# Running streams: rotary queries and new rows padded with zeros to 128 rows, the latent product's heads by turns, the short-conv state stored in one piece

## The chip, the cores and the metric

The kernel runs on one core of one Trainium2 chip. The metric is device time in microseconds (us), from the first to the last instruction with what the launch adds around them; a median of runs stands for a kernel. The core has five engines with their own instruction queues: TensorE (PE in the rows; PEld is its weight load), VectorE (DVE), ScalarE (ACT), GpSimd (POOL) and SyncE (SP), and 16 DMA engines that all queues share.

## The reference, cut to what matters

Two layers of a streaming encoder. Each has three token mixers beside each other (latent attention, a Conformer convolution, a short gated convolution), merged by gates, then an MLP. There are 512 tokens of a new stream (the prompt) and 8 running streams with 16 new tokens each; a running stream attends to 512 cached keys and its own 16 new ones:

```
q_lat = einsum('bqhd,chd->bqhc', q_nope, w_uk)                 # the latent product
s = (einsum('bqhc,bkc->bhqk', q_lat, ckv) + einsum('bqhr,bkr->bhqk', q_rope, krope)) * scale
p = softmax(s)
o_lat = einsum('bhqk,bkc->bqhc', p, ckv)                       # 512 cached rows + 16 new rows
z = gc * h;  new_sc = concat(past_sc, z)[:, -2:]               # state of the short convolution
```

With 8 heads and 16 tokens, a running stream has 128 queries. A query has 256 latent numbers and 32 rotary numbers. `new_sc` are the last two rows of 256 channels, for the prompt and for each of the 8 running streams: 9 x 2 numbers for a channel.

## The kernel before, in words

All activations lie with channels on the 128 partitions. A matmul contracts over partitions: the stationary operand is loaded as weights, the moving one streams through. Dense products are split in a high and a low fp32r part and done in three matmuls (`mm3`, lines 430 to 446: high by high, high by low, low by high, lines 437, 439, 441). Plain fp32 matmuls (values, transposes) count as two instructions each.

Weights come through `Stream` (line 175): a group of up to 512 KB is loaded by SP (line 204), cut by ACT into `wh` (line 226) and by DVE into `wl` (line 227). One group is loaded ahead of the one in use.

The part around the change is the stage of the running streams, once in each layer: 186 to 285 us in layer 0 and from about 1182 us in layer 1. Before it come the prompt's 32 attention steps (loop of line 850). The last 8 of these also do `absorb` (line 821), the latent product: 16 plain matmuls with 64 rows, one at each `yield`, two yields in a step with a transpose between them. Four of them fill one bank of PSUM (`o`, line 829); the fourth is followed by a split of the bank by ACT and DVE into the two parts of `qlh` and `qll`.

In the stage the order of PE is the order of the code, and so is SP's; ACT, DVE and POOL are ordered by a planner that simulates the program, where functions marked `first` have precedence. For each stream b:

- `score_s(b)` (line 923): two halves of 264 keys. Each half takes nine matmuls: six over 128 rows (the two latent halves) and then three over 32 rows, the rotary part. The rotary queries of four streams lie on the four bands of 32 partitions of one tile (`qsr`, split at line 971 into `qsrh` and `qsrl`), and the matmul takes the band of stream b of the queries and of the rotary keys (`rg`, line 927). Then maximum (DVE), exponential (ACT), normalisation (DVE).
- `turn_s(b)` (line 943): transposes of the probabilities, into a tile `spT` of five blocks; the fifth has only 16 rows, for the new keys.
- `value_s(b)` (line 956): for two halves of the latent channels, four matmuls over 128 cached rows (line 962) and one over the 16 new rows (line 963) from `cnew`, a tile of 16 partitions that `new_rows` (line 914) fills for two streams.
- `cut_keys(b)` (line 891): splits the loaded keys (`kT`, `kR`) into two parts and starts the load for stream b + 2; `rows_of` (line 884) loads the value rows `kM`.

Between them run "fills": steps of the dense products `gc1`, `h1`, `gb0`, `gb1` (`side_tile`, line 575). A tile has two halves of eight steps, and a half takes the only bank `D0` of this stage; it is read out by ACT (line 591) or DVE (lines 596, 598, 600) before the next half begins. A stream has 3 fills before `turn_s` and 5 after it. 8 fills come ahead of the loop, after `score_s(0)`, so the order at the start is `score_s(0)`, half of `gc1`, `score_s(1)`, the other half of `gc1`.

`side_out` (line 588) also stores the short-conv state: when a tile `h` is done (for c = 0 just ahead of the stage, for c = 1 within it), POOL issues two DMAs from `Z` (lines 608 and 609), one for the prompt (2 numbers on each partition) and one for the running streams (8 pieces of 2 numbers on each partition).

Of the kernel before, what the change touches and what calls it, by code (L numbers as in the profile page):

```python
# [19 lines left out]
P = 128  # L20
D = 1024
KT = D // P
SEQ = 512
# [297 lines left out]
def trunk(tc, A, O):  # L321
# [54 lines left out]
    def split(h, lo, src, scale=None):  # L376

        return (nc.scalar.activation(out=h, in_=src, func=AF.Copy),
                nc.vector.tensor_tensor(out=lo, in0=src, in1=R(h), op=ALU.subtract))
# [19 lines left out]
    def mm_tile(name, n=HF, ps="D0"):  # L399
        b = banks[ps]  # L400
        return (b[0] if ps == "op" else b).tile([P, 512], F32, tag="mm", name=name)[:, :n]
# [42 lines left out]
    def mm3(*a, **k):  # L444
        for _ in mm3_steps(*a, **k):
            pass
# [61 lines left out]
    for l in range(DEPTH):  # L508
# [48 lines left out]
        Z = pf.tile([P, 2, 2 + SEQ + NB * (2 + NQ)], F32, name="Z")  # L557
        ZP = Z[:, :, 0:2 + SEQ]
        ZS = Z[:, :, 2 + SEQ:].rearrange("p c (b n) -> p c b n", b=NB)

        nc.gpsimd.memset(U[:, :, 0:CH], 0.0)
        nc.gpsimd.memset(Z[:, :, 0:2], 0.0)
# [25 lines left out]
        def side_out(n, c, i, a, b, t, o):  # L588
            q = lambda z: z[:, SEQ:].rearrange("p (b q) -> p b q", b=NB)
            if n == "ca" or n == "gc":  # L590
                nc.scalar.activation(out=t[:, a:b], in_=o, func=AF.Copy, scale=0.5 if n == "ca" else 1.0)
            elif n == "cg":
                nc.scalar.activation(out=t[:, a:b], in_=o, func=AF.Tanh, scale=0.5)
            elif n == "h":
                g, e = held["gc"], min(b, SEQ)
                nc.vector.tensor_tensor(out=ZP[:, c, 2 + a:2 + e], in0=o[:, :e - a], in1=g[:, a:e], op=ALU.mult)
                if b > SEQ:
                    nc.vector.tensor_tensor(out=ZS[:, c, :, 2:], in0=o[:, SEQ - a:].rearrange("p (b q) -> p b q", b=NB), in1=q(g), op=ALU.mult)
            else:
                nc.vector.tensor_tensor(out=sco[:, c, a:b], in0=o, in1=sco[:, c, a:b], op=ALU.mult)  # L600
            if n == "cg" and i:
                ca = held["ca"]
                nc.vector.scalar_tensor_tensor(out=UP[:, c, CH:], in0=t[:, :SEQ], scalar=1.0, in1=ca[:, :SEQ], op0=ALU.add, op1=ALU.mult)
                nc.vector.scalar_tensor_tensor(out=US[:, c, :, CH:], in0=q(t), scalar=1.0, in1=q(ca), op0=ALU.add, op1=ALU.mult)
                nc.gpsimd.dma_start(O["conf"][l][:, c, 0, :], UP[:, c, SEQ:])
                nc.gpsimd.dma_start(O["conf"][l][:, c, 1:, :], US[:, c, :, NQ:])
            elif n == "h" and i:
                nc.gpsimd.dma_start(O["sc"][l][:, c, 0, :], ZP[:, c, SEQ:])
                nc.gpsimd.dma_start(O["sc"][l][:, c, 1:, :], ZS[:, c, :, NQ:])
                taps_z.append(c)  # L610

        def short_conv(c):
# [208 lines left out]
        def absorb():  # L821

            wukT = pq.tile([P, 4, KL], F32, tag="wuk", name=f"wukT{l}", bufs=1)
            nc.gpsimd.dma_start(wukT, A["w_ukT"][l])
            yield
            qll_h.extend(pq.tile([P, 2, NB, NH, NQ], F32R, tag="qn", name=f"ql{n}{l}", bufs=2) for n in "hl")
            for ct in range(2):
                for e in range(2):
                    o = mm_tile(f"qlat{l}{ct}{e}", 512)
                    for pr in range(4):  # L830
                        nc.tensor.matmul(o[:, pr * P:(pr + 1) * P], wukT[64 * e:64 * e + 64, pr, ct * P:(ct + 1) * P], qsn[64 * e:64 * e + 64, pr, :], start=True, stop=True)
                        if pr == 3:
                            src = o.rearrange("p (r b q) -> p b r q", r=4, b=NB)
                            dh, dl = (t[:, ct].rearrange("p b (r e) q -> p b r e q", e=2)[:, :, :, e, :] for t in qll_h)
                            first(split)(dh, dl, src)
                        yield
# [37 lines left out]
        with pool(f"ps{l}", side="right") as ps:  # L874
# [11 lines left out]
                nc.sync.dma_start(kM[b], A["ckvM"][l, b])  # L886


            raw_k, kM, cn, kt_s, kr_s, late = {0: keys_of(0), 1: keys_of(1)}, {}, {}, {}, {}, {}

            def cut_keys(b):
                kT, kR = raw_k.pop(b)
# [13 lines left out]

            rows_of(0)
            rows_of(1)
            qsrh = ps.tile([P, 2, NH, NQ], F32R, name="qsrh")
            qsrl = ps.tile([P, 2, NH, NQ], F32R, name="qsrl")  # L910
            olat = pq.tile([P, 2, NH, NB, NQ], F32, tag="qr", name=f"olat{l}", bufs=1)

            @first
            def new_rows(b):
                o = psT.tile([P, 512], F32, tag="t", name=f"cn{l}{b}")
                cn["t"] = cnew = pq.tile([NQ, 2, KL], F32, tag="wuk", name=f"cnew{l}{b}", bufs=1)
                for j in range(2):
                    for ct in range(2):
                        nc.tensor.transpose(o[:NQ, j * KL + ct * P:j * KL + (ct + 1) * P], ckv[:, ct, SEQ + (b + j) * NQ:SEQ + (b + j + 1) * NQ], ident)
                nc.vector.tensor_copy(cnew, o[:NQ, :].rearrange("p (b c) -> p b c", b=2))  # L920

            @first
            def score_s(b):
                kTh, kTl = kt_s.pop(b)
                kRh, kRl = kr_s[b // 4]
                s = banks["s"].tile([P, 1024], F32, tag="s", name=f"ss{l}{b}")
                rg = slice(DR * (b % 4), DR * (b % 4) + DR)
                ql = [(qlh[:, 0, b], qll[:, 0, b]), (qlh[:, 1, b], qll[:, 1, b]), (qsrh[rg, b // 4], qsrl[rg, b // 4])]

                for c in range(2):  # L930
                    kk = slice(c * NK // 2, (c + 1) * NK // 2)
                    mm3([s[:, 512 * c:512 * c + NK // 2]], ql, [([kTh[:, 0, kk], kTh[:, 1, kk], kRh[rg, kk]], [kTl[:, 0, kk], kTl[:, 1, kk], kRl[rg, kk]])])
                s2 = s.rearrange("p (c n) -> p c n", c=2)[:, :, :NK // 2]
                st = ps.tile([P, 4], F32, tag="st", name=f"sst{l}{b}", bufs=2)
                pb = ps.tile([P, NK], F32, tag="p", name=f"sp{l}{b}", bufs=2)
                nc.vector.tensor_reduce(out=st[:, 0:1], in_=s2, axis=AX.XY, op=ALU.max, negate=True)
                nc.scalar.activation(out=pb.rearrange("p (c n) -> p c n", c=2), in_=s2, func=AF.Exp, bias=st[:, 0:1], scale=1.0, accum_out=st[:, 1:2])
                nc.vector.reciprocal(out=st[:, 2:3], in_=st[:, 1:2])
                late["i"] = nc.vector.tensor_scalar(out=pb, in0=pb, scalar1=st[:, 2:3], scalar2=None, op0=ALU.mult)
                late[b] = pb  # L940

            @first
            def turn_s(b):
                pb = late[b]
                pT = ps.tile([P, 5, P], F32, tag="pT", name=f"spT{l}{b}", bufs=2)
                tp = psT.tile([P, 512], F32, tag="t", name=f"stp{l}{b}")
                for kt in range(4):
                    nc.tensor.transpose(tp[:, kt * P:(kt + 1) * P], pb[:, kt * P:(kt + 1) * P], ident)
                nc.scalar.activation(out=pT[:, 0:4, :], in_=tp.rearrange("p (k q) -> p k q", k=4), func=AF.Copy)
                tq = psT.tile([P, 512], F32, tag="t", name=f"stq{l}{b}")  # L950
                nc.tensor.transpose(tq[:NQ, :P], pb[:, PAST:], ident)
                nc.vector.tensor_copy(pT[:NQ, 4, :], tq[:NQ, :P])
                late[b] = pT

            @first
            def value_s(b):
                pT = late.pop(b)
                o = mm_tile(f"ol{l}{b}", 512, "op")
                for ct in range(2):
                    oo = o[:, ct * P:(ct + 1) * P]  # L960
                    for kt in range(4):
                        nc.tensor.matmul(oo, kM[b][:, kt, ct * P:(ct + 1) * P], pT[:, kt, :], start=kt == 0, stop=False)
                    nc.tensor.matmul(oo, cn["t"][:, b % 2, ct * P:(ct + 1) * P], pT[:NQ, 4, :], start=False, stop=True)
                nc.vector.tensor_copy(olat[:, :, :, b, :], o[:, :2 * P].rearrange("p (c h q) -> p c h q", c=2, h=NH))
                if b + 2 < NB:
                    rows_of(b + 2)

            i_h, i_l = first(cut_keys)(0)
            with tc.issue_after(i_h.ins):
                nc.scalar.activation(out=oT[:, 3, :SEQ], in_=pv["o"], func=AF.Copy)  # L970
            split(qsrh, qsrl, qsr)
            with tc.issue_after(i_l.ins):
                new_rows(0)
            score_s(0)
# [3 lines left out]
            for b in range(NB):  # L978
# [12 lines left out]
                value_s(b)  # L991
                if b == 2:
                    cut_keys(4)
                if b % 2 and b < NB - 1:
                    new_rows(b + 1)
                for _ in range(SB[2]):
# [483 lines left out]
```

## Time and profile before

| | |
|---|---|
| median of 3 runs | 2011.75 us (2009.53 to 2013.53) |
| profiled execution, its own time | 2013.47 us |
| its span, first to last instruction | 2011.6 us |
| granted clock of TensorE, mean | 0.992 |
| PE busy | 1981.9 us (99%) |
| DVE, ACT, POOL busy | 1343.5, 943.1, 26.1 us |
| stage of the running streams, layer 0 (186 to 285 us) | PE busy 92.11 of 99.00 us, granted clock 0.97 |

A timeline row has start, duration, engine, line, operation, out<-in, shapes; "x8" means that eight instructions are merged. The square bracket is the idle time ahead of it and what ended that. Matmuls are pipelined, so a duration is longer than the step from one start to the next. A granted clock of 1.00 is 2.4 GHz, 0.50 is 1.2 GHz.

### The profile page before, as it was taken

The page shows a single profiled execution, that of the slowest core. Times are in us where ns is not written, and L with a number is a line of the kernel's source. Part 1 is how long each engine was busy: PE and PEld are TensorE (multiplying, and loading weights), DVE is VectorE, ACT ScalarE, POOL GpSimd, SP SyncE. Part 2 cuts the span into 40 slices and gives each one's busy share as a digit, 9 for nine tenths or more (in the row PEclk, how much of TensorE's full clock was granted, in tenths as well). Part 3 has the DMA queues.
Part 4 walks back from the last instruction along what each step waited for, and adds up shares of the span by engine and source line. Part 5 has one row for each costly group of instructions (what it writes and reads, how often), then busy time and mean ns, then how long its engine had stood idle before and what let it go on. Part 6 is the DMA issues. An engine that isn't in the chain of part 4 may idle for free.

```text
span 2011.6 us, 33112 instructions
## 1 busy us (share of the span) xinstructions
PE 1981.9 (99%) x13264; PEld 1908.5 (95%) x13264; DVE 1343.5 (67%) x2922; ACT 943.1 (47%) x1862; POOL 26.1 (1%) x47
## 2 busy tenths in 40 slices
PE   9999999999999999999999999999999999999997
PEld 9887899999999999999997878999999999999997
DVE  5764559867576656776777545697765776667675
ACT  5563322234464555446456532222454655553473
POOL 0000000000000000000000000000000000000000
PEclk9999999999999999999999989999999999999998
DMA  6113322213212333213341034222222223332242
GB/s 201 51 35 90 111 87 79 77 54 96 72 53 95 126 126 116 84 64 105 117 143 65 25 95 113 79 77 79 65 83 64 74 85 121 120 116 85 63 124 76
DMA packets 59882, 180.61 MB, mean 90 GB/s; under 512 B 10544, under 2 KB 13024, under 8 KB 59728
## 3 DMA queue, kind: packets, MB, share of 16 engines
q1 hardware_dynamic: 57472, 172.01, 27.3%
q0 software_dynamic: 2256, 6.48, 1.1%
q8 instruction: 104, 1.70, 0.4%
q14 instruction: 50, 0.41, 0.1%
HBM read 173.78 MB, written 4.69 MB: 89 GB/s over the span
## 4 chain that ended last, share of the span: by engine, by line
PE 94%; DMA 2%; ACT 2%; DVE 1%; issue 0%; SPq 0%; ACTq 0%; DVEq 0%
PE f L441 7%; PE f L439 7%; PE f L437 7%; PE mm_g L437 6%; PE mm_g L439 6%; PE mm_g L441 6%; PE op L814 2%; DMA raw<-in_W_dram 2%; PE mix L437 2%; PE mix L439 2%; PE mix L441 2%; PE C L437 2%; PE B L441 2%; PE C L441 2%; PE C L439 2%; PE B L437 2%
## 5 line engine op out<-in xcount | busy, mean ns | idle before, releaser
L226 ACT ACTIVATE wh<-raw 128x1024 fp32r<-128x1024 f32 (+3 forms) x170 | 166.6, 980 | 298.9 <-PE mm_g L439 201.2
L227 DVE TENSOR_TENSOR wl<-raw,wh 128x1024 fp32r<-128x1024 f32 (+3 forms) x170 | 191.0, 1124 | 123.8 <-ACT wh L226 123.4
L439 PE MATMUL f<-hl,wh 128*128 128x320 f32 x992 | 252.0, 309 | 0.0
L441 PE MATMUL f<-hh,wl 128*128 128x320 f32 x992 | 251.6, 309 | 0.0
L437 PE MATMUL f<-hh,wh 128*128 128x320 f32 x992 | 249.5, 309 | 0.0
L437 PE MATMUL mm_g<-xh,wh 128*128 128x320 f32 x768 | 181.9, 311 | 0.0
L441 PE MATMUL mm_g<-xh,wl 128*128 128x320 f32 x768 | 181.0, 309 | 0.0
L439 PE MATMUL mm_g<-xl,wh 128*128 128x320 f32 x768 | 180.5, 309 | 0.0
L439 PEld LDWEIGHTS f<-hl,wh 128*128 128x128 f32 x992 | 172.5, 188 | 0.0
L441 PEld LDWEIGHTS f<-hh,wl 128*128 128x128 f32 x992 | 172.4, 188 | 0.0
L437 PEld LDWEIGHTS f<-hh,wh 128*128 128x128 f32 x992 | 171.9, 188 | 0.0
L1058 DVE SCALAR_TENSOR_TENSOR cv<-U,vec,cv 128x320 f32<-128x320 f32 x360 | 133.9, 432 | 0.0
L437 PEld LDWEIGHTS mm_g<-xh,wh 128*128 128x128 f32 x768 | 129.7, 188 | 1.5 <-issue 0.3
L441 PEld LDWEIGHTS mm_g<-xh,wl 128*128 128x128 f32 x768 | 129.6, 188 | 0.2
L439 PEld LDWEIGHTS mm_g<-xl,wh 128*128 128x128 f32 x768 | 129.4, 188 | 0.3
L412 DVE TENSOR_TENSOR r<-r,f 128x320 f32<-128x320 f32 x192 | 85.4, 482 | 57.3 <-PE f L441 56.7
L226 ACT ACTIVATE wh<-sm 128x1024 fp32r<-128x1024 f32 x56 | 59.3, 1060 | 122.0 <-DVE sm L261 42.6
L227 DVE TENSOR_TENSOR wl<-sm,wh 128x1024 fp32r<-128x1024 f32 x56 | 68.4, 1222 | 49.1 <-PE C L441 28.8
L437 PE MATMUL mix<-mgh,wh 128*128 128x320 f32 x256 | 79.2, 311 | 0.0
L439 PE MATMUL mix<-mgl,wh 128*128 128x320 f32 x256 | 78.7, 309 | 0.0
L441 PE MATMUL mix<-mgh,wl 128*128 128x320 f32 x256 | 75.2, 309 | 0.0
L226 ACT ACTIVATE wh<-rx 128x1024 fp32r<-128x1024 f32 x28 | 29.6, 1059 | 88.7 <-PE f L439 76.9
(430 smaller groups left out, 5139.5 us busy)
## 6 DMA issues: line engine op xcount, KB each, us to landing
raw<-in_W_dram SPq DMA_DIRECT2D x204, 512.0 KB, 3.6
rx<-in_W_dram SPq DMA_DIRECT2D x28, 512.0 KB, 3.6
rxb<-in_W_dram SPq DMA_DIRECT2D x28, 512.0 KB, 3.7
kT<-in_ckvT_dram SPq DMA_DIRECT2D x16, 512.0 KB, 7.2
kM<-in_ckvM_dram SPq DMA_DIRECT2D x16, 512.0 KB, 4.5
raw<-in_W_dram SPq DMA_DIRECT2D x18, 384.0 KB, 3.0
raw<-in_W_dram SPq DMA_DIRECT2D x12, 256.0 KB, 2.7
x<-in_xT_dram SPq DMA_DIRECT2D x8, 320.0 KB, 5.8
```

Source lines behind the costliest of these rows:

```text
L226: nc.scalar.activation(out=wh[:, :n], in_=src, func=AF.Copy)
L227: nc.vector.tensor_tensor(out=wl[:, :n], in0=src, in1=R(wh[:, :n]), op=ALU.subtract)
L412: nc.vector.tensor_tensor(out=r[i][:, m, :], in0=r[i][:, m, :], in1=o, op=ALU.add)
L437: nc.tensor.matmul(o, wh, h[k], start=st, stop=False, skip_group_check=more)
L439: nc.tensor.matmul(o, wh, lo[k], start=False, stop=False, skip_group_check=more)
L441: nc.tensor.matmul(o, wl, h[k], start=False, stop=sp, skip_group_check=more)
L814: nc.tensor.matmul(op[r0:r0 + 64, qt * P:(qt + 1) * P], vt[kt // 2][:, kt % 2, h * 64:(h + 1) * 64], pT[:, kt * P:(kt + 1) * P], start=kt ...
L1058: nc.vector.scalar_tensor_tensor(out=o, in0=u, scalar=tap, in1=o, op0=ALU.mult, op1=ALU.add)
```

## The change

Four edits, all used in both layers.

1. Rotary queries. `qsrh` and `qsrl` go. Two tiles `qz` of 128 x 4 x 128 are set to zero once a layer by ACT; `rope_q(g)` splits the band j of the queries of group g into block j, so that block j holds stream j's queries on its own 32 partitions and zeros elsewhere. `rope_q(0)` stands where the split stood, `rope_q(1)` behind `cut_keys(4)`. The score takes all 128 rows of block b % 4 and of the rotary keys.
2. New rows. `cnew` becomes a 128-row tile, set to zero by POOL once a layer, of which `new_rows` overwrites the first 16 rows; the probabilities of the new keys go to `spN`, two 128 x 128 tiles set to zero by POOL. Line 963's matmul takes 128 rows. `cnew` and one of the two `spT` tiles share the buffer that held `wukT`, so they can be written after the last matmul of the latent product.
3. Latent product. Two banks are open at once and the heads of a pair alternate; there is still one matmul at each `yield`.
4. Short-conv state. POOL copies both pieces into a tile `zo` (128 x 2 x 9 x 2), and after c = 1 one DMA stores it.

```diff
+        zo = pf.tile([P, 2, 1 + NB, 2], F32, name="zo")
...
-                nc.gpsimd.dma_start(O["sc"][l][:, c, 0, :], ZP[:, c, SEQ:])
-                nc.gpsimd.dma_start(O["sc"][l][:, c, 1:, :], ZS[:, c, :, NQ:])
+                nc.gpsimd.tensor_copy(zo[:, c, 0, :], ZP[:, c, SEQ:])
+                nc.gpsimd.tensor_copy(zo[:, c, 1:, :], ZS[:, c, :, NQ:])
+                if c:
+                    nc.gpsimd.dma_start(O["sc"][l], zo)
...
-                for e in range(2):
-                    o = mm_tile(f"qlat{l}{ct}{e}", 512)
-                    for pr in range(4):
+                os = [mm_tile(f"qlat{l}{ct}{e}", 512) for e in range(2)]
+                for pr in range(4):
+                    for e, o in enumerate(os):
...
-            qsrh = ps.tile([P, 2, NH, NQ], F32R, name="qsrh")
-            qsrl = ps.tile([P, 2, NH, NQ], F32R, name="qsrl")
+            wz = pq.tile([P, 8 * P], F32, tag="wuk", name=f"wz{l}", bufs=1)
+            cnew = wz[:, :2 * KL].rearrange("p (b c) -> p b c", b=2)
+            spT = [wz[:, 2 * KL:].rearrange("p (k q) -> p k q", k=4), ps.tile([P, 4, P], F32, name="spT1")]
+            spN = [ps.tile([P, P], F32, name=f"spN{i}") for i in range(2)]
+            qz = [ps.tile([P, 4, P], F32R, name=f"qz{n}") for n in "hl"]
+            nc.gpsimd.memset(cnew, 0.0)
+            for t in spN:
+                nc.gpsimd.memset(t, 0.0)
+            for z in qz:
+                nc.scalar.activation(out=z, in_=cnew.rearrange("p b (j q) -> p (b j) q", j=2), func=AF.Copy)
+
+            @first
+            def rope_q(g):
+                for j in range(4):
+                    rg = slice(DR * j, DR * j + DR)
+                    split(qz[0][rg, j, :], qz[1][rg, j, :], qsr[rg, g].rearrange("p h q -> p (h q)"))
...
-                rg = slice(DR * (b % 4), DR * (b % 4) + DR)
-                ql = [(qlh[:, 0, b], qll[:, 0, b]), (qlh[:, 1, b], qll[:, 1, b]), (qsrh[rg, b // 4], qsrl[rg, b // 4])]
+                ql = [(qlh[:, 0, b], qll[:, 0, b]), (qlh[:, 1, b], qll[:, 1, b]), (qz[0][:, b % 4], qz[1][:, b % 4])]
...
-                    mm3([s[:, 512 * c:512 * c + NK // 2]], ql, [([kTh[:, 0, kk], kTh[:, 1, kk], kRh[rg, kk]], [kTl[:, 0, kk], kTl[:, 1, kk], kRl[rg, kk]])])
+                    mm3([s[:, 512 * c:512 * c + NK // 2]], ql, [([kTh[:, 0, kk], kTh[:, 1, kk], kRh[:, kk]], [kTl[:, 0, kk], kTl[:, 1, kk], kRl[:, kk]])])
...
-                nc.vector.tensor_copy(pT[:NQ, 4, :], tq[:NQ, :P])
+                nc.vector.tensor_copy(pN[:NQ], tq[:NQ, :P])
...
-                    nc.tensor.matmul(oo, cn["t"][:, b % 2, ct * P:(ct + 1) * P], pT[:NQ, 4, :], start=False, stop=True)
+                    nc.tensor.matmul(oo, cnew[:, b % 2, ct * P:(ct + 1) * P], pN, start=False, stop=True)
...
-            split(qsrh, qsrl, qsr)
+            rope_q(0)
...
                 if b == 2:
                     cut_keys(4)
+                    rope_q(1)
```

## Rows read from the trace of the kernel before

**Rows 1.** The page, part 1: busy time, share of the span, instructions.
```profile
PE 1981.9 (99%) x13264; PEld 1908.5 (95%) x13264; DVE 1343.5 (67%) x2922; ACT 943.1 (47%) x1862; POOL 26.1 (1%) x47
```
**Rows 2.** Timeline of PE, layer 0: `score_s(0)`, `value_s(0)` to `score_s(2)`, and 270.7 us.
```profile
189.01 0.39 PE L437 MATMUL ss<-kRh,qsrh 32*128 32x264 f32 x1
...
208.49 1.05 PE L962 MATMUL ol<-spT,kM 128*128 128x128 f32 x8
...
211.62 0.29 PE L439 MATMUL ss<-kTl,qlh 128*128 128x264 f32 x1
...
212.10 0.28 PE L441 MATMUL ss<-kTh,qll 128*128 128x264 f32 x1
212.31 0.38 PE L437 MATMUL ss<-kRh,qsrh 32*128 32x264 f32 x1
...
214.60 0.32 PE L439 MATMUL mm_h<-xl,wh 128*128 128x320 f32 x1
...
270.73 0.31 PE L441 MATMUL mm_gb<-xh,wl 128*128 128x320 f32 x1
270.88 0.46 PE L437 MATMUL mm_g<-xh,wh 128*128 128x320 f32 x2
```
**Rows 3.** Instructions of line 963, both layers: minimum, median, maximum in ns.
```profile
L963 PE MATMUL ol<-spT,cnew x64: 270/321/372, 209.5 to 1279.5; 16*128 16x128 f32 x64
```
**Rows 4.** Waits of PE, 182 to 285 us: total us, times, longest.
```profile
PE mm_gc L437 <- ACT gcs L591: 5.0, 1, 5.0
PE ss L439 <- DVE kTl L379: 0.7, 1, 0.7
PE mm_gb L437 <- DVE sco L600: 0.6, 1, 0.6
```
**Rows 5.** Waits of PE, 1177 to 1290 us (layer 1).
```profile
PE mm_gc L437 <- ACT gcs L591: 2.0, 1, 2.0
PE stq L951 <- DVE cnew L920: 1.0, 1, 1.0
PE mm_gb L437 <- DVE sco L600: 1.0, 1, 1.0
```
**Rows 6.** Stretches: us, busy of each engine, PEclk, DMA share, GB/s.
```profile
192.00:193.00 1.00, 1.00 (x9) 1.00 (x8) 0.14 (x1) 0.00 (x0) 0.00 (x0) 1.00 0.58 41
198.00:199.00 1.00, 0.00 (x0) 0.00 (x0) 0.00 (x0) 0.05 (x1) 0.00 (x0) 1.00 1.08 424
205.00:206.00 1.00, 1.00 (x6) 0.96 (x5) 0.62 (x2) 0.20 (x2) 0.00 (x0) 0.50 0.37 135
...
1186.00:1190.00 4.00, 4.00 (x16) 3.52 (x15) 1.54 (x7) 0.00 (x0) 0.00 (x0) 0.50 0.68 42
```
**Rows 7.** The page, part 6: DMA issues, KB each, median us to landing.
```profile
raw<-in_W_dram SPq DMA_DIRECT2D x204, 512.0 KB, 3.6
...
out_conf_dram<-U POOLq DMA_DIRECT2D x4, 15.0 KB, 1.7
...
out_sc_dram<-Z POOLq DMA_DIRECT2D x4, 8.0 KB, 7.4
```
**Rows 8.** Timeline of ACT, layer 0, around the end of the long wait.
```profile
201.45 1.06 ACT L226 ACTIVATE wh<-raw 128x1024 fp32r<-128x1024 f32 x1 [0.73 <-DMA raw<-in_W_dram]
202.41 0.42 ACT L591 ACTIVATE gcs<-mm_gc 128x320 f32<-128x320 f32 x1
```
**Rows 9.** Timelines of DVE, POOL and SP, layer 0: single rows.
```profile
183.91 0.42 DVE L379 TENSOR_TENSOR qsrl<-qsr,qsrh 128x256 fp32r<-128x256 f32 x1
...
189.28 0.16 DVE L899 COPY kT<-ckv 128x32 f32<-128x32 f32 x1
...
0.74 0.15 POOL L561 MEMSET U<- 128x60 f32 x1 [0.29 <-POOLq L1456]
...
187.08 0.54 POOL L608 DMA_DIRECT2D out_sc_dram<-Z  x1 [35.78 <-DVE Z L598]
...
191.23 0.59 SPq L204 DMA_DIRECT2D raw<-in_W_dram  x1
```

More of the change, by code (lines that the diff above doesn't have):

```diff
@@ L886, in rows_of @@
                 nc.sync.dma_start(kM[b], A["ckvM"][l, b])
-            raw_k, kM, cn, kt_s, kr_s, late = {0: keys_of(0), 1: keys_of(1)}, {}, {}, {}, {}, {}
+            raw_k, kM, kt_s, kr_s, late = {0: keys_of(0), 1: keys_of(1)}, {}, {}, {}, {}
             def cut_keys(b):
@@ L915, in new_rows @@
                 o = psT.tile([P, 512], F32, tag="t", name=f"cn{l}{b}")
-                cn["t"] = cnew = pq.tile([NQ, 2, KL], F32, tag="wuk", name=f"cnew{l}{b}", bufs=1)
                 for j in range(2):
@@ L919, in new_rows @@
                         nc.tensor.transpose(o[:NQ, j * KL + ct * P:j * KL + (ct + 1) * P], ckv[:, ct, SEQ + (b + j) * NQ:SEQ + (b + j + 1) * NQ], ident)
-                nc.vector.tensor_copy(cnew, o[:NQ, :].rearrange("p (b c) -> p b c", b=2))
+                nc.vector.tensor_copy(cnew[:NQ], o[:NQ, :].rearrange("p (b c) -> p b c", b=2))
             @first
@@ L944, in turn_s @@
                 pb = late[b]
-                pT = ps.tile([P, 5, P], F32, tag="pT", name=f"spT{l}{b}", bufs=2)
+                pT, pN = spT[b % 2], spN[b % 2]
                 tp = psT.tile([P, 512], F32, tag="t", name=f"stp{l}{b}")
@@ L948, in turn_s @@
                     nc.tensor.transpose(tp[:, kt * P:(kt + 1) * P], pb[:, kt * P:(kt + 1) * P], ident)
-                nc.scalar.activation(out=pT[:, 0:4, :], in_=tp.rearrange("p (k q) -> p k q", k=4), func=AF.Copy)
+                nc.scalar.activation(out=pT, in_=tp.rearrange("p (k q) -> p k q", k=4), func=AF.Copy)
                 tq = psT.tile([P, 512], F32, tag="t", name=f"stq{l}{b}")
                 nc.tensor.transpose(tq[:NQ, :P], pb[:, PAST:], ident)
-                nc.vector.tensor_copy(pT[:NQ, 4, :], tq[:NQ, :P])
-                late[b] = pT
+                nc.vector.tensor_copy(pN[:NQ], tq[:NQ, :P])
+                late[b] = pT, pN
             @first
             def value_s(b):
-                pT = late.pop(b)
+                pT, pN = late.pop(b)
                 o = mm_tile(f"ol{l}{b}", 512, "op")
```

## The prediction

> **What bounds the kernel now.** I read part 1 of the page first: TensorE is busy 99% of the span, no other engine over 67% [rows 1]. So a change is worth what it takes off PE's own queue, either matmul time or PE's waits. The next views are those of the stage that the change touches: the timeline of PE, for the step from one matmul's start to the next, and PE's waits there. Outside the stage PE runs without gaps, so what the stage gains reaches the end in full.
>
> **Padding the rows (edits 1 and 2).** Between two 128-row matmuls of a score the step is 0.12 us: four steps lie between 211.62 and 212.10 [rows 2]. From the last of them to the first 32-row matmul it is 0.21 us (212.10 to 212.31). In the value part eight 128-row instructions, the last of which lasts 0.27 us as the shortest of line 963 does [rows 3], give a step of (1.05 - 0.27) / 7 = 0.11 us. The 0.21 us is one part of what a change of row count costs; another part falls on the step behind it. So I take the whole: from 208.49 (first matmul of `value_s(0)`) to 214.60 (second fill behind `score_s(2)`) pass 6.11 us. In it are 20 value instructions, 18 of the score and one fill. At 0.112, 0.12 and 0.147 us (the fill's step is 0.15 from 270.73 to 270.88) that is 2.24 + 2.16 + 0.15 = 4.55 us. The rest, 1.56 us, is spread over eight changes between 128 and 32 or 16 rows, 0.2 us each: into and out of the rotary part for two key halves, into and out of the new rows for two channel halves. Half of these coincide with the end of an accumulation and a new bank, but that alone costs nothing: from 270.73 to 270.88 PE goes from one product and bank to the next at the ordinary step.
>
> With padding every matmul has 128 rows. The count stays, and so does the step: the smallest duration of a 16-row instruction, 0.27 us [rows 3], is that of the 128-row ones. 8 streams in 2 layers: 16 x 1.56 = **25.0 us** saved. (Line 963's 64 instructions are 2 x 2 x 16 [rows 3].)
>
> The Trainium skill, TensorEngine Tiling (Array Packing), says under Key Properties that a change of tiling mode drains TensorE, which is the 0.2 us seen here, but also that tiles on different rows run in parallel, so that a short contraction is to be kept short. By the first the sum is as above, by the second padding would cost time; the second is a rival below.
>
> **The store in one piece (edit 4).** PE's longest wait in the stage is 5.0 us in layer 0, 2.0 us in layer 1: the second half of `gc1` waits until ACT has read the only bank `D0` [rows 4, 5]. ACT was free for it, but line 591 stands in its queue behind `wh` of the next group, which ACT could start only at 201.45, when the load landed [rows 8]. SP had issued this load at 191.23 [rows 9]: 10.2 us, against a median of 3.6 us for loads of its size [rows 7]. In between the DMA engines are occupied (share 0.58) but move 41 GB/s; at 198 they move 424 [rows 6]. POOL had issued the two state stores at 187.08 and just behind [rows 9]; the second, 8 KB in pieces of 8 bytes, takes 7.4 us to land, while a store of 15 KB in pieces of 120 bytes takes 1.7 [rows 7]. So the small pieces hold up the key loads, and these and the weights land late.
>
> After the change nothing is stored at the stage's start; one store of 128 pieces of 144 bytes comes after `h1`. Then the load issued at 191.2 lands about 3.6 to 4 us later, at 195. `wh` (1.06 us) and line 591 (0.42 us) follow [rows 8], to about 196.7. PE is done with `score_s(1)` at 191.3 + 24 x 0.147 + 18 x 0.12 = 197.0. The wait goes, by a margin of 0.3 us. What is late next is then PE itself. The second store delayed loads in the same way two streams later, and I count the waits on `sco` and `cnew` to it (0.6 us in layer 0, 1.0 and 1.0 in layer 1 [rows 4, 5]), which come when DVE and ACT queues stand behind a late `wh`. Waits: 5.0 + 0.6 + 2.0 + 1.0 + 1.0 = **9.6 us**.
>
> Behind the long wait the granted clock is 0.50, the 1.2 GHz level, still in the stretch 205 to 206 [rows 6]. PE restarts at 202.8 (end of line 591 [rows 8]): 3.1 us at half speed lose 1.5 us. Layer 1 I estimate the same: **3.0 us** in all. Layer 1 has a second such stretch, 1186 to 1190 [rows 6], behind the short wait on `kTl` at the stage's start; that wait stays, so I leave this.
>
> **What is added at the stage's start.** POOL's zeros of `cnew` and ACT's two zero copies wait for the last matmul of the latent product. For 128 x 512 on POOL there is no near row: 128 x 60 takes 0.15 us [rows 9], which bounds it from below, and eight and a half times that, 1.3 us, from above. The two ACT copies cost under 1.06 us each [rows 8]. They lie beside PE's last fills before the stage, and the first rotary matmul stands at 189.0 [rows 2], so I cost these at nothing; if that cover is gone they are a rival below. DVE has no cover: `score_s(0)` waits 0.7 us for `kTl` [rows 4], then for `kRl`. Four subtractions of 32 x 128 take the place of one of 128 x 256 (0.42 us). By the 128 x 32 copy (0.16 us) the balance is 4 x 0.16 - 0.42 = +0.2 us, by the 128 x 256 row itself 4 x 0.42 - 0.42 = +1.3 us [rows 9]; 128 numbers lie between, and I take 0.75 us a layer, **1.5 us**. `rope_q(1)` has the 6 us from the end of `score_s(3)` to `score_s(4)`, in which DVE has about 2 us to spare: nothing; without that cover some 1 us a layer. POOL's small copies stand on an engine that is busy 26.1 us in all [rows 1], and what waits behind them is the one store.
>
> **The heads by turns (edit 3).** 16 matmuls, 16 yields and a transpose or fill between any two, as before: no change of row count is saved or added. Two banks fill together, so two splits come close to each other where one came; they end before the bank is needed again (2 to 3 us later). Nothing, with up to 0.5 us each way for each of the two bank pairs of a layer.
>
> **The sum**, against the profiled execution's own 2013.47 us: -25.0 - 9.6 - 3.0 + 1.5 = -36.1, so 1977.4 us. The median of the runs is 1.7 us lower than that execution, which gives 1975.7, said as **1976 us**.
>
> **Rivals.**
> - *The DMA gap stays* (something else in the queues makes it, or ACT's new order keeps a late `wh` ahead of the bank). For: the kernel's order of ACT is planned anew. Against: 41 GB/s begins with the stores and ends with them. Then the waits and the clock stay (12.6 us), and what two scores save ahead of the wait, 2 x 0.79 us a layer, is lost in it: 25.0 - 3.2 = 21.8 us saved, start hidden: 1990 us.
> - *The zeros come late.* POOL runs in order; if the copies to `zo`, which need `Z` (187.08 [rows 9]), stand ahead of the zeros, the rotary queries of stream 0 are ready at 187.1 + 0.2 + 0.6 to 1.3 + 2 x 0.6 to 1.06 + some 1.5, so 190.6 to 192.2, 1.6 to 3.2 us after 189.0, and PE may fall to the half clock as layer 1 did. Some 3 to 6 us a layer with it: 1983 us. For: the copies come first in the code. Against: `Z` is not ready when the zeros are.
> - *Short rows were overlapped* (slower). If 32- and 16-row matmuls ran beside their neighbours, each would take a full step once padded: 16 x (6 x 0.12 + 4 x 0.11) = 18.6 us more, with nothing of the 25.0 saved: 2013.5 + 18.6 - 12.6 + 1.5 - 1.7 = 2019 us. It decides as soon as the overlap is worth more than the 11 us that the waits still bring. Against: ten small matmuls hidden would leave 29 steps, 3.4 us, between 208.49 and 214.60, not 6.11 [rows 2]. This is the second half of that page's rule; the trace does not agree with it for matmuls that follow each other on the same rows.
> - *The changes of row count cost only the visible first step* (0.1 us each, the rest being group ends): 12.5 us saved there instead of 25.0: 1988 us. Against: the step at 270.73.
>
> **How the numbers follow.** Forecast 0.70; gap stays 0.10; late zeros 0.12; half price 0.04; short rows overlapped, or several new waits like the 5.0 us one, 0.04. The likeliest gives 1976 us. Its own lower end: start at +0.2 instead of 0.75 a layer (1.1 us), layer 1's second half-clock stretch gone (2 to 3 us): 1971; upper end with 1.3 us a layer and half clock in layer 0: 1981. The range goes on to take in late zeros, half price and the gap: 1969 to 1991 us. Under 0.2% (4 us) this measurement can't tell from no change. Faster 0.95, same 0.02, slower 0.03.
>
> **What would show it.** Right: the step into the rotary matmuls 0.12 instead of 0.21 us; from the first value matmul of a stream to the second fill behind the next score 4.6 instead of 6.1 us; no DMA stretch near 40 GB/s at the stage's start; no wait of PE on line 591; the clock at 1.00 there. Wrong: 128-row rotary matmuls at steps over 0.12, a wait of PE on `qz`, loads that still take 10 us, or a new wait of several us in the streams' stage.

## The result, and the profile after

The changed kernel takes 1980.06 us (median of 4 runs, 1979.2 to 1981.21) against 2012.13 us before (median of 4 runs): a ratio of 0.9842, 95% interval 0.9825 to 0.986. Forecast were 1976 us with a range of 1969 to 1991, so the direction and the range held and the number was 4 us too low. The profiled execution is that of 1979.2 us, span 1977.4 us, 34.3 us below the one of before. One execution of edit 4 alone (below) took 5911.87 us, three times as long as all others, and is left out of every number.

Part 1 of the page after, beside [rows 1]: PE is busy 28 us less with as many instructions, and no other engine is busy over 68%.

```profile
PE 1953.8 (99%) x13264; PEld 1898.1 (96%) x13264; DVE 1349.3 (68%) x2936; ACT 949.8 (48%) x1880; POOL 24.7 (1%) x55
```

The timeline of PE after, layer 0, `value_s(0)` and `score_s(2)`, the same stretch as in [rows 2] (start, duration, line, out<-in, shapes):

```profile
203.47 1.05 PE L980 MATMUL ol<-wz,kM 128*128 128x128 f32 x8
204.36 0.39 PE L981 MATMUL ol<-spN,wz 128*128 128x128 f32 x2
...
206.30 0.28 PE L441 MATMUL ss<-kTh,qll 128*128 128x264 f32 x1
206.42 0.28 PE L437 MATMUL ss<-kRh,qzh 128*128 128x264 f32 x1
...
207.89 0.32 PE L437 MATMUL mm_h<-xh,wh 128*128 128x320 f32 x1
208.04 0.31 PE L439 MATMUL mm_h<-xl,wh 128*128 128x320 f32 x1
```

In the value part, 0.89 us for eight instructions (204.36 - 203.47) is the ordinary step of 0.11 us. The step into the rotary part is 206.42 - 206.30 = 0.12 us, as between any two matmuls; it was 0.21 us. From the first value matmul to the second fill pass 4.57 us instead of 6.11: 1.54 us a stream, where 1.56 were forecast.

PE's waits in the stage after, first layer 0 (182 to 270 us), then layer 1 (1163 to 1251 us): total us, times, longest. They answer to [rows 4, 5].

```profile
PE ss L439 <- DVE kTl L379: 2.5, 1, 2.5
PE mm_gc L437 <- ACT gcs L592: 0.5, 1, 0.5
```
```profile
PE ss L439 <- DVE kTl L379: 2.5, 1, 2.5
PE ss L439 <- DVE kRl L379: 0.2, 1, 0.2
```

The waits of 5.0 and 2.0 us on `gcs` and those on `sco` and `cnew` are gone. The wait on `kTl` at the start has grown from 0.7 to 2.5 us in each layer. The timeline of DVE there, layer 0, shows why:

```profile
186.90 1.22 DVE L379 TENSOR_TENSOR qzl<-qsr,qzh 32x128 fp32r<-32x128 f32 x4
188.15 1.26 DVE L379 TENSOR_TENSOR kTl<-kT,kTh 128x1056 fp32r<-128x1056 f32 x1
```

The four subtractions of `rope_q(0)` stand directly ahead of the one that PE waits for. Behind the wait PE runs at the lower level of its clock (0.50, 1.2 GHz). Stretches after, layer 0 and layer 1 (us, busy of PE, PEld, DVE, ACT, POOL, granted clock, DMA share, GB/s), beside [rows 6]:

```profile
189.00:192.00 3.00, 2.54 (x11) 2.54 (x12) 2.99 (x7) 0.00 (x0) 0.00 (x0) 0.50 0.49 127
...
205.00:206.00 1.00, 1.00 (x11) 1.00 (x10) 0.10 (x1) 0.00 (x0) 0.00 (x0) 1.00 0.00 0
1172.00:1175.00 3.00, 3.00 (x15) 3.00 (x15) 2.33 (x8) 0.79 (x2) 0.00 (x0) 0.50 0.73 202
190.00:191.00 1.00, 1.00 (x7) 1.00 (x6) 1.00 (x3) 0.00 (x0) 0.00 (x0) 0.50 0.61 47
```

At 205 to 206, half clock before, it is now full. But one stretch near 40 GB/s remains (190 to 191 us), with no store in flight.

**Where the time went.** For every profiled execution I cut out the stage of the running streams (from the start of the first transposition `cn` to the start of the first matmul `uv` behind the stage; after, 186.23 to 269.84 and 1167.26 to 1250.82 us). From its length I take PE's waits inside and what the clock lost outside these waits (the sum over that time of 1 minus the granted clock; half clock while PE waits costs nothing more); the rest is PE's own stepping. Both layers together, in us:

| kernel | length | waits | clock | steps |
|---|---|---|---|---|
| before | 201.8 | 12.0 | 6.7 | 183.1 |
| after | 167.2 | 5.7 | 3.1 | 158.3 |
| difference | -34.6 | -6.2 | -3.6 | -24.8 |

The stage's 34.6 us are the whole difference of the two executions (34.3).

### The profile page after: what moved, and what is told of

It is laid out like the page before. It is cut to its first block, busy times and chain, and to the rows that moved or that the text cites. A ratio compares the mean times of both kernels' runs of the same rounds, so it can differ in the third digit from the quotient of the medians.

```text
span 1977.4 us, 33150 instructions
## 1 busy us (share of the span) xinstructions
PE 1953.8 (99%) x13264; PEld 1898.1 (96%) x13264; DVE 1349.3 (68%) x2936; ACT 949.8 (48%) x1880; POOL 24.7 (1%) x55
## 4 chain that ended last, share of the span: by engine, by line
PE 96%; ACT 2%; DVE 1%; DMA 0%; issue 0%; ACTq 0%; DVEq 0%
PE f L441 8%; PE f L439 8%; PE f L437 8%; PE mm_g L437 6%; PE mm_g L441 6%; PE mm_g L439 6%; PE op L817 2%; PE mix L437 2%; PE mix L439 2%; PE mix L441 2%; PE B L441 2%; PE C L437 2%; PE B L439 2%; PE C L441 2%; PE A L437 2%; PE C L439 2%
```

## The experiments

Three groups were run, each beside the kernel before, whose median there was 2008.08, 2007.18 and 2008.0 us (2012.13 on the chip of the result); the first and the third group ran on one chip. So a kernel is compared through its ratio to the kernel before, or with one from its own chip.

### Each edit alone

**Edit 4 alone**, in two groups; its trace is from the second. In all four kernels of this part the probabilities and new rows lie in the buffers of the changed kernel; where edit 2 isn't in, the matmul takes their first 16 rows only.

```diff
-                nc.gpsimd.dma_start(O["sc"][l][:, c, 0, :], ZP[:, c, SEQ:])
-                nc.gpsimd.dma_start(O["sc"][l][:, c, 1:, :], ZS[:, c, :, NQ:])
+                nc.gpsimd.tensor_copy(zo[:, c, 0, :], ZP[:, c, SEQ:])
+                nc.gpsimd.tensor_copy(zo[:, c, 1:, :], ZS[:, c, :, NQ:])
+                if c:
+                    nc.gpsimd.dma_start(O["sc"][l], zo)
```

> The kernel before with edit 4 alone (the short-conv state stored in one piece; rotary queries, new rows and latent product as before). Theory (the small pieces of the state store hold up the loads behind them): the waits of PE on the one bank go (5.0 and 2.0 us), as do those on sco and cnew (0.6, 1.0, 1.0 us) and most of the half clock behind the long wait (some 3 us), so 12.6 us less, about 2000 us; no stretch near 40 GB/s from 189 to 197 us. Rival (the gap has another cause, or ACT's order keeps the late load ahead of the bank): no change, about 2012 us, and the wait on line 591's copy stays at 2 to 5 us.

> The store in one piece alone, once more, for its trace. Theory A (its waits and half clock go as in the whole change, but PE's waits at the start of the stage stay, and nothing else): 1995 us from a before of 2007.5, wait on line 591 under 1 us. Theory B (the load lands early but the bank, the splits and the weights still come late, because two of the three stretches are made by PE's own order): wait on line 591 2 to 4 us, 2000 us.

Measured: 2001.46 us (median of eight executions, 1996.02 to 2005.56), ratio 0.9963 (0.995 to 0.9977), and the second time 2003.52 us, 0.9972 (0.996 to 0.9984): by the ratios 7.4 and 5.6 us gained, less than both theories gave the second time and somewhat over half of what was expected the first time. **Edit 1 alone** and **edit 2 alone** keep the old store; edit 1's padding of the queries and edit 2's of the new rows are those of the diff ahead of the prediction.

> The kernel before with edit 1 alone (rotary queries padded to 128 rows). Theory (0.2 us for each change of row count): 16 x 0.79 = 12.6 us off the scores. Of this the first two scores of each layer (3.2 us) are lost in the long wait, which the old store keeps, and the four subtractions ahead of kTl on VectorE delay that wait's end by about 1.25 us a layer (2.5 us): net 7 us less, about 2005 us. Rival (half price, 0.1 us for each change): 6.3 - 1.6 - 2.5 = 2 us less, about 2010 us. Rival (short rows were overlapped): slower, over 2018 us.

> The kernel before with edit 2 alone (new rows and their probabilities padded to 128 rows). Theory: 16 x 0.77 = 12.3 us less, all of it behind the long wait, about 2000 us; 2.25 us for the 20 instructions of a value part instead of 2.9. Rival (half price): 6 us less, about 2006 us. Rival (short rows were overlapped): slower.

Measured: 2002.01 us for the queries, ratio 0.9965 (0.9952 to 0.9978), and 2002.21 us for the new rows, 0.9966 (0.9954 to 0.9977). By the ratios these are 7.0 us, as expected, and 6.8 us where 12.3 were expected. The second number is near the rival's 6 us, but the steps below aren't those of half price. **Edit 3 alone:**

```diff
-                for e in range(2):
-                    o = mm_tile(f"qlat{l}{ct}{e}", 512)
-                    for pr in range(4):
+                os = [mm_tile(f"qlat{l}{ct}{e}", 512) for e in range(2)]
+                for pr in range(4):
+                    for e, o in enumerate(os):
```

> The kernel before with edit 3 alone (the latent product's heads by turns). Theory: no change of row count is saved, 2012 us within 1 us. Rival (matmuls on different row halves run beside each other once they alternate): the 32 matmuls' changes of row count or their steps shrink, 3 to 10 us less.

Measured: 2009.1 us, ratio 1.0003 (0.9994 to 1.0013): nothing, as expected.

The single gains are 5.6 to 7.4, 7.0, 6.8 and 0 us, some 20 together; the changed kernel gained 30.1 us on the same chip (1977.94 us, ratio 0.985, 0.9836 to 0.9864, in the last group). The same account of the stage shows what is additive and what isn't. There is no trace of the kernel before from this chip; edit 3 alone, with the same time, stands for it:

| kernel (this chip) | length | waits | clock | steps |
|---|---|---|---|---|
| edit 3 alone | 196.9 | 7.8 | 6.4 | 182.7 |
| edit 4 alone | 191.3 | 2.0 | 6.8 | 182.4 |
| edit 1 alone | 193.3 | 15.4 | 6.5 | 171.4 |
| edit 2 alone | 191.8 | 11.0 | 10.0 | 170.9 |
| all four | 166.4 | 5.0 | 3.4 | 158.0 |

Steps nearly add up: 11.3 us less by edit 1 (12.6 expected), 11.8 by edit 2 (12.3 expected), 23.1 together, and 24.7 in the whole change. Waits and clock don't: edit 1 alone waits 7.6 us more (1.4 of it on `kTl` at the start), and edit 2 alone waits 3.2 us more and loses 3.6 more to the clock. With the old store PE, now faster, runs into the late loads. The waits of edit 2 alone, layer 0:

```profile
PE mm_gc L437 <- ACT gcs L591: 4.1, 1, 4.1
PE mm_gb L437 <- DVE sco L600: 2.2, 1, 2.2
...
```

The wait on `sco`, two streams on, is the place of the second store; it was 0.6 us before [rows 4] and takes back what the streams ahead of it saved. Behind it PE restarts at half clock. My estimate for these two kernels counted only what is lost ahead of the first wait.

Edit 4 alone does the opposite: its trace has no wait on `gcs` or `sco` at all (5.8 us of waits less than with edit 3 alone), but its clock loses 6.8 us, no less than the 6.4 there. The stage's start in that kernel, timeline of PE and a stretch:

```profile
187.97 0.36 PE L437 MATMUL ss<-kTh,qlh 128*128 128x264 f32 x1 [0.30 <-DVE Z L599]
189.04 0.39 PE L439 MATMUL ss<-kTl,qlh 128*128 128x264 f32 x1 [0.71 <-DVE kTl L379]
...
190.69 0.59 PE L437 MATMUL ss<-kTh,qlh 128*128 128x264 f32 x1
191.07 0.42 PE L439 MATMUL ss<-kTl,qlh 128*128 128x264 f32 x1
```
```profile
193.00:197.00 4.00, 4.00 (x16) 3.76 (x16) 2.58 (x5) 1.76 (x3) 0.00 (x0) 0.50 0.72 247
```

PE steps at half clock from 190.7 to 197.4 us behind two pauses of 0.30 and 0.71 us. So theory A was right on the waits and wrong on the clock, and theory B's waits of 2 to 4 us weren't there. The clock also differs between executions of this one kernel: in the first group its mean went from 0.994 (2005.56 us) to 0.998 (1996.02 us), and the traced execution has 0.994. The 0.004 between them are 8 us of 2000, most of the 9.5 us by which the two differ. At 0.998 the gain is 12.1 us, near the 12.6 first expected, so what edit 4 gives alone depends on how much half clock an execution happens to have.

### The paddings with the old store

The changed kernel with the two old stores of `Z` in place of `zo` (the diff of edit 4, undone).

> The changed kernel with edit 4 undone (state stored in small pieces again). Theory: the long wait on the one bank comes back in both layers and with it the half clock; what padding saved ahead of it is lost in it: 1980 + 10 to 13 us, about 1991 us. Rival (the store is not the cause): 1980 us.

Measured: 1993.05 us, ratio 0.9936 (0.9921 to 0.995). Against the kernel of the same group that pads to 96 rows and runs like the changed one (next part) that is 15.1 us more. Its waits in layer 0:

```profile
PE mm_gb L437 <- DVE sco L600: 3.0, 1, 3.0
PE mm_gc L437 <- ACT gcs L591: 2.6, 1, 2.6
PE ss L439 <- DVE kTl L379: 2.5, 1, 2.5
...
```

In its account (length 180.6, waits 16.4, clock 4.8, steps 159.4 us) the steps are within 1.5 us of the 96-row kernel's 157.9, the waits 11 us more. The store gains 5.6 to 7.4 us alone and 15 us once the paddings are in. This is the rival of the staying gap, made on purpose. It was priced at 1990 us, a gain of 21.8; this kernel gains 14.1 us over the kernel before of its group (2007.18).

Edit 4 changes the moment of the first store as well as its pieces. The second store tells the two apart, since both kernels have one there: at 222.21 us in the changed kernel, at 225.29 and 225.83 with the old store. The load of weights issued some 2.5 us behind it, first in the changed kernel (at 224.79), then with the old store (at 228.34); KB, us to landing:

```profile
raw<-in_W_dram SPq DMA_DIRECT2D x1, 512.0 KB, 7.1
```
```profile
raw<-in_W_dram SPq DMA_DIRECT2D x1, 512.0 KB, 12.7
```

So with a store at the same place the load takes 5.6 us longer behind small pieces. Whether their number, their size or the second DMA does it wasn't tried.

### How many rows

Only line 981's matmul, with 64 or 96 of its 128 rows:

```diff
-                    nc.tensor.matmul(oo, cnew[:, b % 2, ct * P:(ct + 1) * P], pN, start=False, stop=True)
+                    nc.tensor.matmul(oo, cnew[:64, b % 2, ct * P:(ct + 1) * P], pN[:64], start=False, stop=True)
```

> The changed kernel with the new rows' matmul over 64 of the 128 padded rows. Theory (a change of the array's row mode costs 0.2 us, however many rows the smaller mode has): all 64 changes of the value part come back, 16 x 0.77 = 12.3 us more, about 1992 us. Rival (the price falls with the rows that are missing): a good half of it, about 1986 us.

> The changed kernel with the new rows' matmul over 96 of the 128 padded rows. Theory (the price is that of another mode of the array, and 96 rows are no mode of their own: the prompt's scores over 96 rows stand beside 128-row matmuls at the ordinary step): same as the changed kernel, 1980 us within 1 us. Rival (any other row count costs): 12 us more, about 1992 us.

Measured: 1990.06 us with 64 rows (ratio 0.9917, 0.9902 to 0.9932), 1977.95 us with 96 (0.9854, 0.9838 to 0.9871), 12.1 us apart. The value part of stream 0, first with 64 rows, then with 96:

```profile
204.11 1.05 PE L980 MATMUL ol<-wz,kM 128*128 128x128 f32 x8
205.09 0.49 PE L981 MATMUL ol<-spN,wz 64*128 64x128 f32 x2
205.51 1.16 PE L980 MATMUL ol<-wz,kM 128*128 128x128 f32 x8
```
```profile
204.49 1.05 PE L980 MATMUL ol<-wz,kM 128*128 128x128 f32 x8
205.38 0.39 PE L981 MATMUL ol<-spN,wz 96*128 96x128 f32 x2
205.60 1.06 PE L980 MATMUL ol<-wz,kM 128*128 128x128 f32 x8
```

Two instructions with 64 rows take 0.42 us to the next start, with 96 rows 0.22. The price isn't graded by rows: 64 cost what 16 did (12.1 us, against 11.8 us of steps by edit 2 alone), 96 nothing. In 2 layers and 8 streams there are 16 x 4 such changes, so 12.1 / 64 = 0.19 us each. The Trainium skill, TensorEngine Tiling (Array Packing), lists under Tiling Modes row modes of 128, 64 and 32, none of 96, and says that a change of mode drains the engine. The price with 64 rows and its absence with 96 agree with that list; that a change is a drain no run here shows.

### The start of the stage

The first group of rotary queries is split later: stream 0's block behind the first cut of the keys, the other three behind the second.

```diff
-            rope_q(0)
-            with tc.issue_after(i_l.ins):
+            with tc.issue_after(i_h.ins), tc.issue_after(i_l.ins):
+                rope_q(0, (0,))
...
-            cut_keys(1)
+            j_h, j_l = cut_keys(1)
+            with tc.issue_after(j_h.ins), tc.issue_after(j_l.ins):
+                rope_q(0, (1, 2, 3))
```

> The changed kernel with the split of the first four streams' rotary queries put behind the split of stream 0's keys on ScalarE and VectorE (block 0), and of stream 1's (blocks 1 to 3). Theory (the missing 4 us are the subtractions that stand ahead of kTl on VectorE, PE's wait behind them and the half clock after it): the wait on kTl falls from 2.5 to about 1 us in each layer, 3 to 6 us less, about 1975 us. Rival (the start only shifts the wait to qz or kRl): within 1 us of 1980.

Measured: 1977.05 us, ratio 0.9855 (0.984 to 0.9869). The only measure in its group is the 96-row kernel with 1977.95 us, which it can't be told from. Its trace has half the wait on `kTl` and one half-clock stretch less (account: waits 3.9, clock 1.7, steps 158.7 us). It was run again with the next edit.

### The same step once more: the latent product

`absorb`'s queries lie in two tiles of 128 rows, each with zeros in the other head's half; the weights take 128 rows.

```diff
-        qsn = pq.tile([P, 4, P], F32, tag="qsn", name="qsn", bufs=1)
+        qsn = [pq.tile([P, 4, P], F32, tag=f"qsn{e or str()}", name=f"qsn{e}", bufs=1) for e in range(2)]
+        for t in qsn:
+            nc.gpsimd.memset(t, 0.0)
...
-                        nc.tensor.matmul(o[:, pr * P:(pr + 1) * P], wukT[64 * e:64 * e + 64, pr, ct * P:(ct + 1) * P], qsn[64 * e:64 * e + 64, pr, :], start=True, stop=True)
+                        nc.tensor.matmul(o[:, pr * P:(pr + 1) * P], wukT[:, pr, ct * P:(ct + 1) * P], qsn[e][:, pr, :], start=True, stop=True)
```

For the room one of four buffers of `pT` goes, and one `spT` tile shares a buffer with the second `qsn`. Three kernels ran together: the changed kernel, this edit on it, and this edit with the later split.

> The changed kernel again, on the chip of the next three, as their measure. 1974 to 1980 us.

> The changed kernel with the same step taken once more: the queries of the latent product, 64 rows so far, in two tiles of 128 rows with zeros in the other half, weights of 128 rows. Theory (a change of row count costs 0.2 us, 64 rows among them): a pair of instructions with 64 rows between two of 128 has 0.14 us too much ahead of it and 0.19 us behind it in the trace of the changed kernel (163.06 to 163.83: 0.36 and 0.41 us for two instructions each, of which 0.22 are steps), 0.33 us a pair; 16 pairs in 2 layers make 10.6 us: some 1966 us, with steps of 0.11 us into line 839's matmuls. Rival (64 rows against 128 is a change that mostly costs the time of a group end): under 3 us. Second rival: doubled copies of the queries on ACT make a new wait before the product, 1 to 2 us of the gain lost.

> As the one before, and the first group of rotary queries split only behind the first cut of the keys (block 0) and behind the second (blocks 1 to 3). Theory of the start (the four subtractions ahead of the keys' cost PE 1.8 us and then a stretch at half clock in layer 0): 2 to 4 us below the one before; rival (the start is hidden in what DVE has to do anyway, PE then waits for the next split): within 1 us of it.

Measured: 1977.94 us for the changed kernel, 1970.06 us (1968.97 to 1971.73; ratio to before 0.9814, 0.98 to 0.9828) with the padded product, 1968.18 us (1967.99 to 1968.83; 0.9805, 0.9791 to 0.9819) with both. Both beat the changed kernel, by 7.9 and 9.8 us. One attention step of layer 0, PE, in the changed kernel and then with the padded product:

```profile
163.06 0.43 PE L817 MATMUL op<-pT,vt 128*64 128x128 f32 x2
163.42 0.48 PE L835 MATMUL qlat<-qsn,wukT 64*128 64x128 f32 x2
163.83 0.44 PE L804 MATMUL tp<-ident,p 128*128 128x128 f32 x2
164.20 0.48 PE L835 MATMUL qlat<-qsn,wukT 64*128 64x128 f32 x2
164.62 0.42 PE L437 MATMUL mm_h<-xh,wh 128*128 128x320 f32 x1
```
```profile
162.88 0.43 PE L821 MATMUL op<-pT,vt 128*64 128x128 f32 x2
163.24 0.49 PE L839 MATMUL qlat<-qsn,wukT 128*128 128x128 f32 x2
163.56 0.38 PE L808 MATMUL tp<-ident,p 128*128 128x128 f32 x2
163.78 0.39 PE L839 MATMUL qlat<-qsn,wukT 128*128 128x128 f32 x2
163.92 0.39 PE L437 MATMUL mm_h<-xh,wh 128*128 128x320 f32 x1
```

From `op` to the dense matmul 1.56 us became 1.04. With 8 such steps in 2 layers that makes 16 x 0.52 = 8.3 us, against 7.9 measured; 10.6 were expected. The missing part is at the first pair: from `op` to line 839 the step stays 0.36 us. There the row count no longer changes, but the columns of the weights do, from 64 to 128. That this costs as a change of rows does is read from these rows alone and wasn't tried.

The later split brings 1.9 us beside the padded product, where 2 to 4 were expected: every run with it is below every run without, though the two ratio intervals overlap. In the account most of it is the clock, which loses 1.7 instead of 3.3 us; the waits are 4.3 instead of 4.8. In layer 0 the start then looks like this (timeline of PE, stretch):

```profile
185.34 0.39 PE L439 MATMUL ss<-kTl,qlh 128*128 128x264 f32 x1 [1.25 <-DVE kTl L379]
...
186.75 0.39 PE L439 MATMUL ss<-kRl,qzh 128*128 128x264 f32 x1 [0.43 <-DVE kRl L379]
```
```profile
186.00:190.00 4.00, 3.57 (x27) 3.37 (x26) 3.84 (x13) 0.91 (x2) 0.00 (x0) 1.00 0.71 179
```

The 2.2 us of wait on `kTl` that the padded product has here without the later split have become 1.25 and 0.43, and the clock stays full. In layer 1 the same two pauses are followed by a half-clock stretch all the same (1.7 us lost there, none in layer 0), and the first kernel with the later split shows the same in both layers. What decides that isn't settled.

## Why the prediction was nearly right

- **Changes of row count, -25.0 us: right.** The steps of the stage fell by 24.8 us, by 24.4 us against edit 4 alone on another chip; per stream 1.54 of 1.56 us. The half price is refuted by the steps, the overlap of short rows by the time, and the 64-row kernel gives 0.19 us a change against the 0.2 of the sum.
- **Waits, -9.6 us: right for this trace.** The five waits of that sum fell to one of 0.5 us; short ones on `Z` and, in layer 0, on `cnew` went with them. That it is the small-piece store is shown by the kernel with both paddings and the old store, where they are back. But the size is that of one execution: in the trace of edit 3 alone, which has the old store and the time of the kernel before, the same waits are 5.2 us. The chain of steps behind the number was looser than the sum: the load of the weights was issued at 192.49 us, 1.26 us later than before, and took 5.3 us instead of 3.6 to 4, so it lands at 197.8 us, not at 195, and leaves that half microsecond.

The timelines of SP and of ACT after, layer 0, where `wh` waits for that load ([rows 8, 9]):

```profile
192.49 0.59 SPq L204 DMA_DIRECT2D raw<-in_W_dram  x1
```
```profile
197.82 1.06 ACT L226 ACTIVATE wh<-raw 128x1024 fp32r<-128x1024 f32 x1 [2.41 <-DMA raw<-in_W_dram]
```

- **The start, +1.5 us: mis-sized.** The durations were right: 1.22 us for the four subtractions, 0.8 more than the old one's 0.42, where I took 0.75. But the difference was the wrong term. The subtraction that went stood at 183.91 [rows 9], 3 us ahead of the place that matters, and cost PE nothing. The new four stand at 186.90, where `kTl`'s stood before, and push it back by all of their time. The first matmul on `kTl` stands 189.46 - 186.23 = 3.23 us behind the stage's first instruction; before it was 188.20 - 186.23 = 1.97 (its row below). So the start cost 1.26 us a layer, 2.5 instead of 1.5 us. The wait itself grew by more, 1.8 us a layer, because PE's first score matmul now stands 0.55 us earlier (186.58 for 187.13) and waits there instead of ahead of it.

The start of the stage in the kernel before, layer 0, timeline of PE:

```profile
186.23 0.60 PE L919 MATMUL cn<-ident,ckv 128*16 128x128 f32 x4
187.13 0.36 PE L437 MATMUL ss<-kTh,qlh 128*128 128x264 f32 x1 [0.30 <-DVE Z L598]
188.20 0.39 PE L439 MATMUL ss<-kTl,qlh 128*128 128x264 f32 x1 [0.71 <-DVE kTl L379]
```

and in the changed kernel:

```profile
186.23 0.60 PE L938 MATMUL cn<-ident,ckv 128*16 128x128 f32 x4
186.58 0.37 PE L437 MATMUL ss<-kTh,qlh 128*128 128x264 f32 x1
189.46 0.59 PE L439 MATMUL ss<-kTl,qlh 128*128 128x264 f32 x1 [2.51 <-DVE kTl L379]
```

- **Half clock, -3.0 us: near in sum, by two errors that cancel.** Outside the waits the clock lost 6.7 us before (1.6 and 5.1 by layer) and loses 3.1 now (1.4 and 1.7): 3.6 us less. The stretches behind the long waits are gone, as forecast. In layer 1 I counted the stretch at the stage's start as staying, 3.4 us; only 1.7 remain. In layer 0, where the start had run at full clock, 1.4 us are new. That the longer wait made them is not shown: with edit 4 alone the start of layer 0 has the short waits of before, 0.30 and 0.71 us, and falls to half clock too.
- **Zeros late: no.** POOL's zeros of `cnew` began at 182.39 us and took 0.53 us (my bounds were 0.15 and 1.3), ahead of the copies to `zo`. PE never waited for `qz`; its wait on `kTl` grew, by DVE's order.
- **Edit 3, nothing: right.**

So the stage gave 34.6 us where the sum had 36.1: the steps brought 0.2 us less, waits and start together 1.9 us less (6.2 for 8.1), the clock 0.6 us more. The rest of the 4 us lies in the last step: I set the median 1.7 us below the profiled execution, and this time it is 0.9 us above it. That the number came within 4 us is luck in part. The profiled execution of before was among the longest of its kernel, and on the chip of the first and third group the same change gained 30.1 us, where the steps fell as forecast (24.7 us) but fewer of the waits were there to be saved.

One sign that I named was wrong: a stretch near 40 GB/s at the stage's start does not by itself mean the store. There is still one (47 GB/s from 190 to 191 us), with no store in flight; what makes it is open. Two more came only in part: PE still waits 0.5 us on `gcs` in layer 0, and the clock, full at 205 us, is 0.50 at the stage's start.

## What to carry to other kernels

Padding a short contraction with zeros to the row count of its neighbours pays where matmuls of other row counts stand between: count the changes in the timeline, not the rows. When an engine is the bound, price step savings by the step, but then look which late transfer the faster engine will meet: here the paddings alone kept little more than half of their gain (14.1 us, with some 23 us of steps saved) until the small-piece store was gone. An operation that replaces another costs its whole duration, not the difference, if the old one stood off the path and the new one on it.

## What the runs showed of the hardware

- A matmul of 96 rows among those of 128 costs no change; one of 64 costs 0.19 us each way, and one of 16 cost about the same (11.8 us of steps for 64 changes, 0.18 each).
- The clock level does not follow from the length of a wait: half clock came behind pauses of 0.30 and 0.71 us (edit 4 alone, both layers) and not behind 1.25 and 0.43 (padded product with the later split, layer 0). In the kernel before, the same two pauses with the same matmuls behind them were followed by full clock in layer 0 and by half clock in layer 1 (192 to 193 and 1186 to 1190 us, [rows 6]).
- The store of 18 KB in 128 pieces of 144 bytes lands after 2.0 us, where 8 KB in pieces of 8 bytes took 7.4 us [rows 7]; a load of weights behind the small pieces took 12.7 us, one behind the store in one piece 7.1. The list of DMA issues after (KB each, median us to landing):

```profile
out_sc_dram<-zo POOLq DMA_DIRECT2D x2, 18.0 KB, 2.0
```
